# Attention loop of a hybrid decoder layer: TensorE's order fixed to the program's, and each step's first scores written ahead of the transposes of the step behind it

## The chip, the cores and the metric

The kernel runs on one core of one Trainium2 chip. The metric is the device time of one execution in microseconds (us), as the median of several runs. Below, PE is TensorE (PEld its weight loads), DVE is VectorE, ACT is ScalarE, POOL is GpSimd and SP is SyncE.

## What is computed

One layer of a decoder on 1024 tokens of width 1024, in float32: a half-step SwiGLU, then two attentions side by side (MLA and FoX, eight heads each), gated and projected, then a second half-step SwiGLU. The part that the change touches is the attention, swept over blocks of 128 queries:

```python
def one_block(i):
    start = i * Q_BLOCK
    q_blk = lax.dynamic_slice_in_dim(q, start, Q_BLOCK, axis=2)
    logits = jnp.einsum('bhqd,bhkd->bhqk', q_blk, k, preferred_element_type=jnp.float32) * scale
    if log_decay_cum is not None:
        c_q = lax.dynamic_slice_in_dim(log_decay_cum, start, Q_BLOCK, axis=2)
        logits = logits + (c_q[..., :, None] - log_decay_cum[..., None, :])
    logits = jnp.where(k_pos[None, :] <= q_pos[:, None], logits, -jnp.inf)
    probs = jax.nn.softmax(logits, axis=-1)
    return jnp.einsum('bhqk,bhkd->bhqd', probs.astype(v.dtype), v)
...
y_mla = mla_mixer(q_lat, kv_lat, k_rope, ...)
y_fox = fox_mixer(fq, fk, fv, f_logit, ...)
mixed = (jax.nn.sigmoid(g_mla + b_gate[l, 0]) * (y_mla @ w_branch_mla[l])
         + jax.nn.sigmoid(g_fox + b_gate[l, 1]) * (y_fox @ w_branch_fox[l]))
x = x + mixed @ w_o[l]
```

## The kernel before, in words

The layer runs as one program in stages: first SwiGLU, input projection, attention, output projection, second SwiGLU. To keep float32 accuracy with fast matmuls, most operands are split into a high and a low part, and a product is made of two or three matmuls.

**The loop.** `attention` (line 1874) has 64 steps: 2 attentions x 8 heads x 4 groups `g` of two query blocks. A step holds

- the scores of its two query blocks (`scores`, line 2010): matmuls into a tile `pss` (three passes for MLA, two for FoX); DVE adds the causal mask on the diagonal block (line 2025) and takes the maximum (line 2027, `nm`), and ACT makes the exponentials and their sum (line 2030) into a slot of `s_act`. The first block, 2g, is called A below, the second, 2g+1, is called B.
- of the step behind it (`later`, line 2033): `g+1` chunks of transposes of the exponentials (line 2049, PE through an identity into a tile `pspt`, seven or eight matmuls for two chunks). Each chunk is split into high and low by ACT and then DVE (`split_sb`, lines 167 and 170, into `s_v`). Then the product with the values (lines 2059 and 2064, tile `pspv`), which ACT copies out and DVE adds (lines 2066 and 2067, `cmb`), and POOL adds into place. The chunks are called T0 to T3 and the product P.
- 12 matmuls (sometimes 24, in three steps none) of other work with tiles `psgate` and `psg`: the input projection of the two gates and, at the end, the MLA branch's projection. Their operands (`op`, `whi`, `wlo`) are split by ACT and DVE in earlier steps, some from sums that POOL makes.
- now and then a small piece: the forget gates' sums (`chain`), the reciprocal of the sums per pair of heads (`finish_pair`, line 2077), loads of the next head by SP.

**Buffers.** PSUM has two tiles for `pss` (two banks each), a ring of three banks for everything from `psb` (`pspt`, `pspv` and small pieces, in the order in which the program asks for them) and one bank for `psg`. So in a step with four chunks, T0 and T1 take two banks of the ring, T2 takes the bank of the product that just ended, once ACT and DVE have copied it out, and T3 takes T0's bank, once it is split.

**The order of the work.** The program's text gives the order of one step before the change: half of the chunks behind, A, the rest of the chunks, B, gate matmuls and other pieces, P. (With one or two chunks all of them go ahead of A.) But a scheduler sets the order on each engine: it takes what is ready by its own estimate, earlier text first, and so it moves single transposes, scores and gate matmuls past each other. In some other stages the kernel fixes an engine's order to the text's with `in_order` (line 127), which makes each instruction of the named engines follow the one that the text has before it, without a semaphore. The attention loop had no such fix.

Of the kernel before, what the change touches and what calls it, by code (L numbers as in the profile page):

```python
# [10 lines left out]
F32 = mybir.dt.float32  # L11
# [8 lines left out]
P = 128  # L20
T = 1024
NT = T // P
# [5 lines left out]
HEADS = 8  # L28
# [24 lines left out]
class Parts:  # L53
# [5 lines left out]
    def at(self, k, s=slice(None)):  # L59
        return self.tiles[k // self.per][:, k % self.per, s]  # L60
# [5 lines left out]
class Layer:  # L66
# [1807 lines left out]
    def attention(self, gates, more, mix):  # L1874


        nc = self.nc
        vbuf = {}
        pbuf = self.parts("act", 4, 2)
        values = self.slot("act", F16, 4096).rearrange("p (b t c) -> p b t c", b=2, t=NT)  # L1880
        self.pcount = 0
        self.rest = None
        ops = {}
        GR = NT // 2

# [24 lines left out]
        for i in (2, 5, 7, 9):  # L1910
            at(i, lambda: next(chain, None))
        pinned = []
        for k, e in ((k, e) for k in (3, 1, 2, 4) for e in range(2)):
            for f, engine in ((sum_of, None), (high, mybir.EngineType.Activation), (low, mybir.EngineType.DVE)):
                pinned.append((engine, lambda f=f, k=k, e=e: f(k, e)))
        for i in range(2 * HEADS * GR):
            for f in jobs.get(i, ()):
                f()
            k, g = divmod(i, GR)
            a, h = divmod(k, HEADS)  # L1920
            j = h % 2
            if g == 0:
                load(k + 1)
                if j == 0:
                    atp = self.ring.tile([P, T], F32, tag="atp", bufs=2, name="atp")
                    rs = self.sm.tile([P, NT, 2], F32, tag="rsum", bufs=2, name="rsum")
            pr = []
            chunks = late[0] if late is not None else []
            half = len(chunks) // 2 if len(chunks) > 2 else len(chunks)
            for f in chunks[:half]:  # L1930
                f()
            pr.append(self.scores(ops[k], 2 * g, j, rs, pbuf))
            for f in chunks[half:]:
                f()
            pr.append(self.scores(ops[k], 2 * g + 1, j, rs, pbuf))
            if i < 57:
                for engine, f in pinned[2 * i - 2:2 * i] if i else ():
                    last = engine and self.latest(engine)
                    f()
                    if last:  # L1940
                        self.follow(last)
                if i == 11:
                    begin(0)
                if i == 13:
                    sums(0)
                while gates and done < (total - 1) * (i + 1) / 57 + (i > 1):
                    gates.pop(0)()
                    done += 1
                if len(gates) <= 6 and pieces:
                    pieces.pop(0)()  # L1950
                if i == 55:
                    prep()
                if i == 56:
                    sig()
            else:
                for _ in range(2 if i % 2 else 1):
                    if len(mla) > 5:
                        mla.pop(0)()
            if self.rest is not None and (i - 1) % GR == 0:
                scaled = self.rest()  # L1960
                self.rest = None
            if scaled is not None and (i - 3) % GR == 0:
                scaled()
                scaled = None
            if i == 2 * HEADS * GR - 3:
                self.make_sel()
                fox = self.at_slots("v")
                for p in range(2):
                    self.split_at(fox, 1, p)
            if i == 2 * HEADS * GR - 1:  # L1970
                self.split_at(fox, 1, 2)
            if late is not None:
                late[1]()
            late = self.later(a, h, g, j, pr, vbuf[k // 2][:, :, j * P:(j + 1) * P], atp, rs)
# [305 lines left out]
```

## Time and profile before

| | us |
|---|---|
| median of 3 runs (2071.18 to 2074.14) | 2073.53 |
| the profiled execution's own time | 2072.48 |
| its span | 2070.7 |
| PE busy in the span | 2027.4 |
| DVE busy in the span | 1502.1 |
| ACT busy in the span | 1184.6 |
| the attention loop's place in the span | 880 to 1301 |

The profile is that of one execution. Lines such as L2049 are lines of the kernel before; a row names line, engine, operation, what is written and read (`out<-in`, with buffer numbers left out), its shape, how often, and busy us. "idle before" is the engine's idle time ahead of the rows' instructions, and the name behind the arrow is what ended it. Matmuls are pipelined, and their ends in the profile are modelled: the next one starts before the one ahead has ended. The granted clock is the share of full speed that PE was given.

### The profile page before, as it was taken

Reading aid. Unit: us, or ns where it says so; the run is one execution under the profiler, and the core shown is the slowest. Engines: PE = TensorE matmul, PEld = TensorE weight load, DVE = VectorE, ACT = ScalarE, POOL = GpSimd, SP = SyncE. Lnnn points to the kernel's source line nnn. Section 1 sums busy time; section 2 is a strip of 40 time slices with the busy share of each in tenths; the row PEclk is TensorE's granted clock in tenths of the full one; section 3 lists DMA queues with packets and bytes.
Section 4 is the critical chain, followed back from the end, with each engine's and each line's share of the span. In section 5 each row is a group of like instructions: output and inputs, shape, how many; then the busy total and the mean of one; then the engine's idle time right before and its main releaser. Section 6 shows DMA issues by size and latency. Waiting matters only on the chain.

```text
span 2070.7 us, 28667 instructions
## 1 busy us (share of the span) xinstructions
PE 2027.4 (98%) x10187; PEld 1101.0 (53%) x10187; DVE 1502.1 (73%) x2514; ACT 1184.6 (57%) x2005; POOL 691.7 (33%) x748
## 2 busy tenths in 40 slices
PE   8999999999999999999999999999999999999999
PEld 4444444444447555566666666478444444444445
DVE  7866666778877789578888888763765555459876
ACT  6666665545564454467777776422566666555552
POOL 4454544752201212123222321000254555564300
PEclk9999999999999999999999999999999999999999
DMA  8248676575534465654455575541554564355433
GB/s 230 76 143 269 201 250 203 177 270 178 171 110 167 135 195 151 179 137 115 133 140 147 147 211 157 189 147 55 134 144 136 185 181 138 122 197 205 143 111 112
DMA packets 271833, 336.00 MB, mean 162 GB/s; under 512 B 21817, under 2 KB 201897, under 8 KB 271690
## 3 DMA queue, kind: packets, MB, share of 16 engines
q1 hardware_dynamic: 271690, 334.18, 52.8%
q8 instruction: 80, 1.31, 0.3%
q14 instruction: 63, 0.52, 0.1%
HBM read 240.32 MB, written 93.81 MB: 161 GB/s over the span
## 4 chain that ended last, share of the span: by engine, by line
PE 77%; DVE 12%; ACT 5%; issue 3%; DMA 2%; SPq 0%; POOL 0%; ACTq 0%; DVEq 0%; POOLq 0%
PE pst L1104 19%; PE psd L1257 15%; PE psb L1104 11%; PE psg L1104 3%; DVE op L170 2%; PE pss L2023 2%; PE psb L159 2%; PE pspt L2049 2%; PE psb L157 2%; PE psb L158 2%; PE psgate L1104 2%; PE pspv L2059 2%; ACT s_act L2030 1%; PE psin L159 1%; PE psin L157 1%
## 5 line engine op out<-in xcount | busy, mean ns | idle before, releaser
L1104 PEld LDWEIGHTS <-op 128*128 128x128 f16 x3780 | 366.4, 98 | 431.6 <-issue 4.0
L1257 PE MATMUL psd<-op 128*128 128x512 f16 x1680 | 364.3, 379 | 1.2 <-DVE s_wd L209 0.8
L1257 PEld LDWEIGHTS <-op 128*128 128x128 f16 x1680 | 164.3, 98 | 199.8 <-issue 2.6
L170 DVE SCALAR_TENSOR_TENSOR op<-s_u,s_v,op 128x512 f16<-128x512 f32 x170 | 151.4, 900 | 90.1 <-ACT op L167 89.8
L1104 PE MATMUL pst<-s_u,op 128*128 128x512 f16 x720 | 165.2, 379 | 1.3 <-DVE s_act L1152 1.3
L1104 PE MATMUL pst<-s_v,op 128*128 128x512 f16 x720 | 165.2, 379 | 1.3 <-DVE s_u L1152 1.3
L167 ACT ACTIVATE op<-s_u,s_v 128x512 f16<-128x512 f32 x170 | 118.0, 714 | 83.8 <-PE psd L1257 71.6
L170 DVE SCALAR_TENSOR_TENSOR op<-s_act,s_wd,op 128x512 f16<-128x512 f32 x130 | 118.5, 924 | 58.7 <-ACT op L167 58.7
L2030 ACT ACTIVATE s_act<-pss,nm 128x128 f32<-128x128 f32 (+7 forms) x128 | 94.7, 740 | 60.7 <-DVE nm L2027 60.1
L2023 PE MATMUL pss<-s_wd 96*128 96x256 f32 (+5 forms) x480 | 122.8, 372 | 0.5 <-ACT s_act L2030 0.2
L2069 POOL COPY atp<-cmb 64x128 f32<-64x128 f32 x64 | 22.6, 353 | 279.7 <-DVE cmb L2067 275.4
L1073 POOL TENSOR_TENSOR sums<-s_u 128x512 f32<-128x512 f32 x20 | 27.6, 1382 | 252.0 <-PE psa L620 157.1
L2049 PE MATMUL pspt<-ident,s_act 128*128 128x128 f32 x576 | 95.1, 282 | 15.4 <-ACT s_act L2030 10.0
L170 DVE SCALAR_TENSOR_TENSOR s_v<-pspt,s_v 128x512 f16<-128x512 f32 (+1 forms) x160 | 95.4, 629 | 9.4 <-ACT s_v L167 8.6
L2027 DVE TENSOR_REDUCE nm<-pss 128x1 f32<-128x128 f32 (+7 forms) x128 | 95.4, 751 | 2.2
L167 ACT ACTIVATE s_v<-pspt 128x512 f16<-128x512 f32 (+1 forms) x160 | 82.6, 552 | 23.0 <-PE pspt L2049 21.2
L167 ACT ACTIVATE op<-s_wd 128x512 f16<-128x512 f32 x70 | 50.4, 721 | 76.3 <-PE psd L1257 73.1
L167 ACT ACTIVATE op<-s_act,s_wd 128x512 f16<-128x512 f32 x130 | 88.8, 710 | 6.7 <-PE pst L1104 4.1
L2049 PEld LDWEIGHTS pspt<-ident,s_act 128*128 128x128 f32 x576 | 66.2, 142 | 47.1 <-ACT s_act L2030 28.8
L2023 PEld LDWEIGHTS pss<-s_wd 96*128 96x128 f32 (+1 forms) x480 | 78.5, 192 | 8.1 <-ACT s_act L2030 1.8
L1104 PE MATMUL psb<-s_wd,op 128*128 128x512 f16 x360 | 82.6, 379 | 0.0
L1104 PE MATMUL psb<-s_u,op 128*128 128x512 f16 x360 | 82.6, 379 | 0.0
(567 smaller groups left out, 4569.7 us busy)
## 6 DMA issues: line engine op xcount, KB each, us to landing
sumd<-s_u SPq DMA_DIRECT2D x20, 1024.0 KB
s_u<-in_w_in_dram SPq DMA_DIRECT2D x19, 1024.0 KB
s_wd<-in_ffn_w_down_dram SPq DMA_DIRECT2D x32, 512.0 KB
sumd<-s_wd SPq DMA_DIRECT2D x13, 1024.0 KB
s_wd<-fd SPq DMA_DIRECT2D x48, 256.0 KB
s_act<-in_ffn_w_down_dram SPq DMA_DIRECT2D x22, 512.0 KB
s_wd<-sumd SPq DMA_DIRECT2D x14, 768.0 KB
s_u<-sumd SPq DMA_DIRECT2D x14, 768.0 KB
```

The costliest lines, as they stand in the source:

```text
L157: mm(out, lhsT=lh, rhs=rh, start=start, stop=False)
L158: mm(out, lhsT=lh, rhs=rl, start=False, stop=False)
L159: mm(out, lhsT=ll, rhs=rh, start=False, stop=stop)
L167: self.nc.scalar.activation(hi, src, AF.Copy, scale=scale)
L170: self.nc.vector.scalar_tensor_tensor(out=lo, in0=src, scalar=scale, in1=hi, op0=ALU.mult, op1=ALU.subtract)
L1104: mm(out, lhsT=a[:, k, :], rhs=b[:, k, :], start=start and k == 0 and i == 0, stop=k == n - 1 and i == 2, skip_group_check=True,)
L1257: nc.tensor.matmul(o, lhsT=u[:, r], rhs=w, start=start and m == 0, stop=k == CK - 1 and m == 2, skip_group_check=True,)
L2023: mm(ps[:, b:e], lhsT=a[:, q], rhs=bb[:, b:e], start=k == 0, stop=k == len(passes) - 1)
L2027: nc.vector.tensor_reduce(out=nm, in_=ps[:, :n], op=ALU.max, axis=AX.X, negate=True)
L2030: nc.scalar.activation(pn[:, :n], ps[:, :n], AF.Exp, bias=nm, accum_out=rs[:, i, j:j + 1])
L2049: nc.tensor.transpose(pt[:, o:o + P], pr[m][:, kt * P:(kt + 1) * P], self.ident)
L2059: mm(po[:, :256], lhsT=v[:, kt, :], rhs=slab[:, s, c, e * 256:(e + 1) * 256], start=kt == 0 and s == 0, stop=False,)
```

## The change

The whole body of the loop goes under `in_order` for PE. So PE's instructions from the first step's to the last step's stand as in the text; DVE, ACT, POOL and SP are still ordered by the scheduler, which now reckons with this order of PE. And the text is changed in one place: A stands ahead of the first half of the chunks, and B ahead of the rest. (With one or two chunks, all of them stand between A and B.) The rest of the body is only indented. The line numbers behind line 1916 grow by one.

```diff
-        for i in range(2 * HEADS * GR):
-            for f in jobs.get(i, ()):
-                f()
...
+        with self.in_order(mybir.EngineType.PE):
+            for i in range(2 * HEADS * GR):
+                for f in jobs.get(i, ()):
                     f()
...
             pr = []
             chunks = late[0] if late is not None else []
             half = len(chunks) // 2 if len(chunks) > 2 else len(chunks)
-            for f in chunks[:half]:
-                f()
-            pr.append(self.scores(ops[k], 2 * g, j, rs, pbuf))
-            for f in chunks[half:]:
-                f()
-            pr.append(self.scores(ops[k], 2 * g + 1, j, rs, pbuf))
...
+                pr.append(self.scores(ops[k], 2 * g, j, rs, pbuf))
+                for f in chunks[:half]:
+                    f()
+                pr.append(self.scores(ops[k], 2 * g + 1, j, rs, pbuf))
+                for f in chunks[half:]:
+                    f()
```

The first place is on PE, in a step with four chunks in the FoX half, from the end of a product on. Numbers tell the tiles apart: `pss_10579` is A, `pss_10599` is B, and T0 and T1 are `pspt_10565` and `pspt_10572`. Before:

```order
L2064 MATMUL pspv_10535<-s_v_10479,s_act_7781 128x256
L2049 MATMUL pspt_10565<-ident_91,s_act_7780 128x128
L2049 MATMUL pspt_10572<-ident_91,s_act_7780 128x128
L2023 MATMUL pss_10579<-s_wd_10263 128x256
L2023 MATMUL pss_10579<-s_wd_10264 128x256
L1104 LDWEIGHTS op_10458
L1104 MATMUL psgate_10518<-s_u_5345,op_10458 128x512
L1104 LDWEIGHTS op_10458
L1104 MATMUL psgate_10518<-s_u_5346,op_10458 128x512
L1104 LDWEIGHTS op_10458
L1104 MATMUL psgate_10518<-s_u_5345,op_10458 128x512
L2049 MATMUL pspt_10565<-ident_91,s_act_7780 128x128 x3
```

Before, one transpose each of T0 and T1 stood ahead of A, and three gate matmuls between A and the rest of T0. The same place after the change (A is now `pss_10565`, B `pss_10586`, T0 to T3 are `pspt_10572`, `pspt_10579`, `pspt_10593` and `pspt_10600`):

```order
L2065 MATMUL pspv_10535<-s_v_10479,s_act_7781 128x256
L2024 MATMUL pss_10565<-s_wd_10263 128x256
L2024 MATMUL pss_10565<-s_wd_10264 128x256
L2050 MATMUL pspt_10572<-ident_91,s_act_7780 128x128 x4
L2050 MATMUL pspt_10579<-ident_91,s_act_7780 128x128 x4
L2024 MATMUL pss_10586<-s_wd_10263 128x256
L2024 MATMUL pss_10586<-s_wd_10264 128x256
L2050 MATMUL pspt_10593<-ident_91,s_act_7780 128x128 x4
L2050 MATMUL pspt_10600<-ident_91,s_act_7780 128x128 x3
L1104 LDWEIGHTS op_10458
L1104 MATMUL psgate_10518<-s_u_5345,op_10458 128x512
```

Now A, T0, T1, B, T2 and T3 follow each other without anything between them, and all gate matmuls stand behind T3.

The second place is on PE too, in one of the three steps without gate matmuls of their own; the rows start in B (`pss_11016`), and the step's product is `pspv_11025`. Before:

```order
L2023 MATMUL pss_11016<-s_wd_10555 128x512
L2023 MATMUL pss_11016<-s_wd_10556 128x512
L2023 MATMUL pss_11016<-s_wd_10555 128x256
L2023 MATMUL pss_11016<-s_wd_10556 128x256
L1104 LDWEIGHTS op_10907
L1104 MATMUL psgate_11078<-s_u_8215,op_10907 128x512
```

Seven gate matmuls of the next step followed here, and then the product. After the change:

```order
L2024 MATMUL pss_11016<-s_wd_10555 128x512
L2024 MATMUL pss_11016<-s_wd_10556 128x512
L2024 MATMUL pss_11016<-s_wd_10555 128x256
L2024 MATMUL pss_11016<-s_wd_10556 128x256
L2060 LDWEIGHTS s_act_7781
L2060 MATMUL pspv_11025<-s_v_10993,s_act_7781 128x256
```

The product now follows B directly, and the gate matmuls stay in the next step.

The third place is on DVE, around the copy of a product (`cmb`) at the start of a step with four chunks. The rows start with the last split of the step before; `pss_10795` is that step's B, `pss_10868` is A. Before:

```order
L170 SCALAR_TENSOR_TENSOR s_v_10765<-pspt_10789,s_v_10765 128x384
L2025 TENSOR_TENSOR pss_10795<-pss_10795,maskb_5607 128x128
L2027 TENSOR_REDUCE nm_10801<-pss_10795 128x1
L2025 TENSOR_TENSOR pss_10868<-pss_10868,maskb_5607 128x128
L2067 TENSOR_TENSOR cmb_10835<-pspv_10823,cmb_10835 64x512
L2027 TENSOR_REDUCE nm_10872<-pss_10868 128x1
L2084 RECIPROCAL rinv_10933<-rsum_10274 128x8x2
L170 SCALAR_TENSOR_TENSOR op_10816<-sums_10622,ws_97,op_10816 128x512
L170 SCALAR_TENSOR_TENSOR op_10819<-s_act_10462,ws_97,op_10819 128x512
L170 SCALAR_TENSOR_TENSOR s_v_10841<-pspt_10854,s_v_10841 128x512
```

The copy stood ahead of the two gate operands (`op`), and these ahead of T0's split. After the change (`pss_10782` is B of the step before, `pss_10854` is A):

```order
L2028 TENSOR_REDUCE nm_10788<-pss_10782 128x1
L170 SCALAR_TENSOR_TENSOR s_v_10765<-pspt_10798,s_v_10765 128x384
L170 SCALAR_TENSOR_TENSOR op_10816<-sums_10622,ws_97,op_10816 128x512
L170 SCALAR_TENSOR_TENSOR op_10819<-s_act_10462,ws_97,op_10819 128x512
L2085 RECIPROCAL rinv_10933<-rsum_10274 128x8x2
L2026 TENSOR_TENSOR pss_10854<-pss_10854,maskb_5607 128x128
L2068 TENSOR_TENSOR cmb_10835<-pspv_10823,cmb_10835 64x512
L2028 TENSOR_REDUCE nm_10858<-pss_10854 128x1
L170 SCALAR_TENSOR_TENSOR s_v_10841<-pspt_10861,s_v_10841 128x512
```

B's maximum moved ahead of the last split, and the two gate operands moved from behind the copy to ahead of it; T0's split now follows the copy and A's maximum.

More of the change, by code (lines that the diff above doesn't have):

```diff
@@ L1915, in attention @@
                 pinned.append((engine, lambda f=f, k=k, e=e: f(k, e)))
-        for i in range(2 * HEADS * GR):
-            for f in jobs.get(i, ()):
-                f()
[L1919 to L1929, printed above, removed]
-            for f in chunks[:half]:
-                f()
-            pr.append(self.scores(ops[k], 2 * g, j, rs, pbuf))
-            for f in chunks[half:]:
-                f()
-            pr.append(self.scores(ops[k], 2 * g + 1, j, rs, pbuf))
-            if i < 57:
-                for engine, f in pinned[2 * i - 2:2 * i] if i else ():
-                    last = engine and self.latest(engine)
-                    f()
[L1940 to L1974, printed above, removed]
@@ new lines, in attention @@
+        with self.in_order(mybir.EngineType.PE):
+            for i in range(2 * HEADS * GR):
+                for f in jobs.get(i, ()):
+                    f()
+                k, g = divmod(i, GR)
+                a, h = divmod(k, HEADS)
+                j = h % 2
+                if g == 0:
+                    load(k + 1)
+                    if j == 0:
+                        atp = self.ring.tile([P, T], F32, tag="atp", bufs=2, name="atp")
+                        rs = self.sm.tile([P, NT, 2], F32, tag="rsum", bufs=2, name="rsum")
+                pr = []
+                chunks = late[0] if late is not None else []
+                half = len(chunks) // 2 if len(chunks) > 2 else len(chunks)
+                pr.append(self.scores(ops[k], 2 * g, j, rs, pbuf))
[4 more added lines that the diff above has]
+                    f()
+                if i < 57:
+                    for engine, f in pinned[2 * i - 2:2 * i] if i else ():
+                        last = engine and self.latest(engine)
+                        f()
+                        if last:
+                            self.follow(last)
+                    if i == 11:
+                        begin(0)
+                    if i == 13:
+                        sums(0)
+                    while gates and done < (total - 1) * (i + 1) / 57 + (i > 1):
+                        gates.pop(0)()
+                        done += 1
+                    if len(gates) <= 6 and pieces:
+                        pieces.pop(0)()
+                    if i == 55:
+                        prep()
+                    if i == 56:
+                        sig()
+                else:
+                    for _ in range(2 if i % 2 else 1):
+                        if len(mla) > 5:
+                            mla.pop(0)()
+                if self.rest is not None and (i - 1) % GR == 0:
+                    scaled = self.rest()
+                    self.rest = None
+                if scaled is not None and (i - 3) % GR == 0:
+                    scaled()
+                    scaled = None
+                if i == 2 * HEADS * GR - 3:
+                    self.make_sel()
+                    fox = self.at_slots("v")
+                    for p in range(2):
+                        self.split_at(fox, 1, p)
+                if i == 2 * HEADS * GR - 1:
+                    self.split_at(fox, 1, 2)
+                if late is not None:
+                    late[1]()
+                late = self.later(a, h, g, j, pr, vbuf[k // 2][:, :, j * P:(j + 1) * P], atp, rs)
```

## The prediction

> **What bounds the kernel now.** I read the page first, then busy time by window over the attention loop, then TensorE's waits there, then its neighbours' durations, and last the timeline of one step. The page's shares of the span:
>
> ```profile
> PE 2027.4 (98%) x10187; PEld 1101.0 (53%) x10187; DVE 1502.1 (73%) x2514; ACT 1184.6 (57%) x2005; POOL 691.7 (33%) x748
> ```
>
> TensorE (PE) has work almost all the time, so the change can win only what PE waits inside the loop. The loop's first and last scores put it at 880 to 1301 us. The window view for that stretch, with its halves (columns: length, busy us and instructions of PE, PEld, DVE, ACT, POOL, granted clock, DMA share, GB/s):
>
> ```profile
> 880.00:1095.00 215.00, 207.71 (x1260) 140.38 (x1259) 175.27 (x309) 151.95 (x307) 62.05 (x112) 0.99 0.50 132
> 1095.00:1301.00 206.00, 195.25 (x1171) 125.71 (x1169) 171.87 (x296) 144.30 (x290) 51.49 (x106) 0.99 0.59 160
> 880.00:1301.00 421.00, 402.96 (x2428) 266.08 (x2427) 347.14 (x605) 296.25 (x596) 113.54 (x218) 0.99 0.54 146
> ```
>
> PE is idle for 421.00 - 402.96 = 18.0 us. VectorE (DVE) works 347.14 us, 82% of the loop and 83% of its second half, so it is the nearest second bound: even without one PE wait, the loop is not much shorter than DVE's queue plus its latencies. The waits that PE and its weight loader (PEld) show in the loop:
>
> ```profile
> PE pspt L2049 <- ACT s_act L2030: 10.0, 15, 2.0
> PE pspt L2049 <- DVE cmb L2067: 2.8, 4, 1.1
> PE pspt L2049 <- DVE s_v L170: 1.1, 1, 1.1
> PEld pspt L2049 <- ACT s_act L2030: 28.8, 55, 2.2
> PEld pspt L2049 <- DVE cmb L2067: 8.6, 15, 1.3
> PEld pspt L2049 <- DVE s_v L170: 3.0, 8, 0.6
> ```
>
> Nearly every wait stands before a transpose (pspt). Three things end it: the exponentials (ScalarE, s_act), the copy of an older product out of the bank that the transpose needs (cmb), and the split of an older transpose (s_v). PE's rows are too low, because a matmul's modelled end covers the start of a wait: a transpose lasts 282 ns in the group below, but starts 0.11 us behind its neighbour (three in 1142.40 to 1142.73 further down). PEld's rows are too high, because it may idle while PE still works. PE's idle time before transposes (15.4 us, next fence) plus 0.16 us for each of the 55 + 15 + 8 = 78 waits gives 15.4 + 12.5 = 28 us. By PEld's shares, 20 us of that wait for exponentials, 6 for cmb, 2 for s_v.
>
> The durations that the steps below use, from the groups by line within the loop (busy us, mean ns | idle before it and what ended it):
>
> ```profile
> L2049 PE MATMUL pspt<-ident,s_act 128*128 128x128 f32 x576 | 95.1, 282 | 15.4 <-ACT s_act L2030 10.0 <-DVE cmb L2067 2.8 <-DVE s_v L170 1.1
> L170 DVE SCALAR_TENSOR_TENSOR s_v<-pspt,s_v 128x512 f16<-128x512 f32 x96 | 63.0, 682 | 8.0 <-ACT s_v L167 7.4
> L2067 DVE TENSOR_TENSOR cmb<-pspv,cmb 64x512 f32<-64x512 f32 x63 | 43.2, 686 | 17.5 <-ACT cmb L2066 16.5
> L2025 DVE TENSOR_TENSOR pss<-pss,maskb 128x128 f32<-128x128 f32 x128 | 36.2, 290 | 18.3 <-PE pss L2023 17.5 <-ACT s_v L167 0.3
> L170 DVE SCALAR_TENSOR_TENSOR s_v<-pspt,s_v 128x384 f16<-128x384 f32 x64 | 35.1, 548 | 1.5 <-ACT s_v L167 1.2
> L170 DVE SCALAR_TENSOR_TENSOR op<-s_act,ws,op 128x512 f16<-128x512 f32 x25 | 18.5, 755 | 9.8 <-ACT op L167 9.6
> L2027 DVE TENSOR_REDUCE nm<-pss 128x1 f32<-128x128 f32 x16 | 4.6, 286 | 0.3
> L2066 ACT COPY cmb<-pspv 64x512 f32<-64x512 f32 x63 | 36.5, 580 | 16.6 <-PE pspv L2064 15.1 <-POOL s_act L1074 0.2
> ```
>
> **The change, part by part.** It adds and removes no work on PE; it moves it. A and B are a step's first and second scores, T0 to T3 the transposed chunks of the step behind, P the product of the step behind. A step with group g has g chunks behind it, or four when g is 0. Before, one step with four chunks on the timeline of PE (start us, us, what, idle time before it):
>
> ```profile
> 1137.36 0.27 PE L2064 MATMUL pspv<-s_v,s_act 128*128 128x256 f16 x1
> 1137.47 0.38 PE L2049 MATMUL pspt<-ident,s_act 128*128 128x128 f32 x2
> 1137.61 0.48 PE L2023 MATMUL pss<-s_wd 128*128 128x256 f32 x2
> 1139.21 1.58 PE L2049 MATMUL pspt<-ident,s_act 128*128 128x128 f32 x10 [1.12 <-DVE cmb L2067]
> 1140.55 0.49 PE L2023 MATMUL pss<-s_wd 128*128 128x256 f32 x2
> 1140.88 1.69 PE L1104 MATMUL psgate<-s_u,op 128*128 128x512 f16 x7
> 1142.40 0.49 PE L2049 MATMUL pspt<-ident,s_act 128*128 128x128 f32 x3
> 1142.73 1.24 PE L1104 MATMUL psgate<-s_u,op 128*128 128x512 f16 x5
> 1143.81 1.69 PE L2059 MATMUL pspv<-s_v,s_act 128*128 128x256 f16 x14
> 1145.34 0.27 PE L2064 MATMUL pspv<-s_v,s_act 128*128 128x256 f16 x1
> ```
>
> The same step on ACT and DVE (the copy's two halves, and B's exponentials):
>
> ```profile
> 1137.73 0.58 ACT L2066 COPY cmb<-pspv 64x512 f32<-64x512 f32 x1 [0.67 <-PE pspv L2064]
> 1138.33 1.11 ACT L2030 ACTIVATE s_act<-pss,nm 128x1024 f32<-128x1024 f32 x1
> 1138.46 0.69 DVE L2067 TENSOR_TENSOR cmb<-pspv,cmb 64x512 f32<-64x512 f32 x1
> ```
>
> From one product's last matmul to the next product's it takes 1145.34 - 1137.36 = 7.98 us. Starts give the spacing: two narrow scores 0.33 us (1140.55 to 1140.88), a gate matmul 0.217 (seven to 1142.40), a transpose 0.11, a product matmul 0.11 (14 in 1.53).
>
> *Scores ahead of transposes.* The order shows that the scheduler had already put A ahead of all but one transpose of a chunk: of T0 and T1 one each went first, which needs only the first exponentials. Moving those is worth at most 0.11 us each while nothing waits. What is new is that B too passes T1 and T2 in steps of three chunks (seven transposes, 0.77 us), so that B's exponentials are asked for 0.77 us earlier before the next product. Of the 20 us of exponential waits that can take all or nothing; B's maximum and exponentials still queue on a DVE that is 82% busy, so I take a third, -7 us, in the steps of one to three chunks (bounds 0 and -20; those of four come next).
>
> *Gate matmuls no longer fill.* Before, the scheduler put 1 to 12 gate matmuls (0.2 to 2.6 us) between A and the transposes, and between T1 and T3, in many steps of four chunks. Now all stand behind T3, where they cover the product's wait for the splits. I work the quoted step out in the new order, from the product's last matmul: 0.11, A 0.33, so T0 is due at 0.44. It needs the exponentials of the last B, which ended at 1138.33 + 1.11 = 1139.44, 2.08 behind the product; 0.77 earlier is 1.31, with the next DVE or ACT piece perhaps ahead of it. T0 waits 0.87. T0 and T1 take 0.88, B 0.33: T2 is due at 1.31 + 0.88 + 0.33 = 2.52. T2 needs the bank of the product just ended: there are three such banks, and T0 and T1 hold the others. The copy ended at 1138.46 + 0.69 = 1139.15, at 1.79; that is the early end, with no wait. In the new order DVE has two gate operands (0.755 each) queued ahead of that copy, and A's mask as before: 3.3 is the late end, a wait of 0.78. T3 needs T0 split: a split of 0.682 and its ACT half behind T0, or the copy, a maximum (0.286) and the split; I count 0.2 to 0.53 for it. Without waits the step takes 0.11 + 0.33 + 0.88 + 0.33 + T2 0.44 + T3 0.33 + twelve gate matmuls 2.6 + fifteen product matmuls 1.65 = 6.67. With them it takes 6.67 + 0.87 + (0 to 0.78) + (0.2 to 0.53) = 7.7 to 8.85, against 7.98: -0.3 to +0.9. Steps of four chunks that had gate matmuls in these gaps waited less before, and can only lose, up to 1.3. Over 16 such steps: -5 to +18 us. I take +0.45 each, +7 us, near the middle.
>
> *Products without gate matmuls in front.* The pacing leaves three loop steps without gate matmuls. The scheduler had pulled some of the next step's forward there; now P follows its last transposes (or B) directly. The last chunk needs its ACT half and then its DVE half (0.548 or 0.682); with copy, mask or maximum in the queue that is 1 to 2.5 us after the transpose, less B or the product's first matmuls. I take 0.8 us each, +2.5 us (bounds +1 and +5).
>
> *Elsewhere.* Outside the loop the order of PE, ACT, DVE, GpSimd and SyncE is unchanged; inside it, the gate operands keep a step's distance to their matmuls, and the loads of the next head are issued at the same place. Nothing.
>
> Sum: -7 + 7 + 2.5 = +2.5 us. The profiled execution took 2072.48 us (span 2070.7), so 2075 on its scale; it is 1.05 us below the median of the three runs, so **2076 us**. A measurement of this kernel can tell about 0.2%, 4.1 us, from no change.
>
> One rule of the trace has to be priced as well, the clock. Two places with clustered waits, each with the stretch ahead of it:
>
> ```profile
> 920.00:930.00 10.00, 8.01 (x42) 5.62 (x41) 6.81 (x10) 5.05 (x9) 2.27 (x6) 0.88 0.57 148
> 923.50:927.55 4.05, 2.06 (x13) 1.68 (x12) 2.18 (x2) 3.84 (x6) 0.00 (x0) 1.00 0.39 93
> 1208.00:1220.00 12.00, 10.25 (x55) 6.92 (x54) 10.14 (x15) 10.28 (x18) 1.15 (x3) 0.86 0.70 221
> 1137.00:1146.00 9.00, 7.83 (x57) 5.71 (x56) 6.82 (x14) 7.15 (x17) 1.16 (x3) 1.00 0.55 115
> ```
>
> When PE worked 2.06 of 4.05 us, the granted clock then fell (0.88 over 10 us, 0.86 over 12: 1.2 to 1.7 us lost). One wait of 1.1 us, as at 1137 to 1146, left it at 1.00. So waits of about 2 us close together cost 1.7 us more; the waits of T0, T2 and T3 lie within 2.5 us of each other, and reach 2.2 us together only at the late end (0.87 + 0.78 + 0.53). I put nothing in the sum for it. [...]
>
> **Rivals.** *The exponential waits go* (faster). If B's 0.77 us and A's place ahead of every transpose are enough, the 20 us shrink to 4, nothing else is lost in the four-chunk steps, and the gate-less products cost 2: -14 us, 2060. For it: the mean wait, 28.8 / 55 = 0.5 us, is shorter than 0.77. Against it: steps of one and two chunks have nearly the same order as before, and DVE's load is unchanged.
>
> *The bank of the last product* (slower). If the copy regularly ends over 2.5 us after its product (the point from which T2 waits for it whatever the exponentials do), the step that is worked out pays 0.9 and those that had cover up to 1.3; at 1.1 each, 16 x 1.1 = 18, plus 3 for the gate-less products, plus 2 for a fall of the clock, less 5 for exponentials: +18 us, 2091. For it: 8.6 us already wait for cmb on PEld, and the new order puts operand splits ahead of that copy. Against it: DVE idled 17.5 us before its cmb, 16.5 of them for ACT's half, so it is often free by then.
>
> **How the numbers follow.** The forecast, waits moved but hardly fewer, 2067 to 2084: 0.42, of which 0.04 lies over 0.2% faster, 0.30 within, 0.08 slower. The exponential waits go: 0.28, all faster. The bank: 0.30, all slower. So faster 0.32, same 0.30, slower 0.38. The likeliest case's own range is 2067 to 2084; to leave out no more than 2 in 10 the range takes in most of both rivals, 2059 to 2092.
>
> **What would show it.** Right: PE's idle time in the loop again 14 to 24 us, with pspt's wait for s_act down from 10.0 and its waits for cmb and s_v up from 2.8 and 1.1 together to about 8; a pspv wait for s_v that hardly existed. The forecast is wrong if the s_act wait is gone and cmb stays (first rival), or if cmb and s_v grow past 20 us or the clock row shows new falls (second).

## The result, and the profile after

The changed kernel takes 2088.63 us (median of 4 runs, 2086.52 to 2091.04), the kernel before 2073.10 on the same chip (4 runs, 2071.18 to 2074.14). The ratio is 1.0077 (95% interval 1.0065 to 1.0090): slower by 15.5 us, more than the 0.2% that can be told from no change. The range of 2059 to 2092 holds it; the likeliest time, 2076, was 12.6 us too low. The profiled execution took 2089.07 us, its span is 2087.2.

The engines' row on the page:

```profile
PE 2026.5 (97%) x10187; PEld 1105.9 (53%) x10187; DVE 1501.3 (72%) x2514; ACT 1187.9 (57%) x2005; POOL 684.3 (33%) x748
```

The window view of the loop, whose last product now starts at 1317.4 instead of 1301.0 (columns as in the prediction):

```profile
880.00:1316.00 436.00, 401.79 (x2422) 270.57 (x2423) 345.92 (x604) 299.15 (x596) 109.15 (x218) 0.99 0.52 141
```

PE does the same work in 2026.5 instead of 2027.4 us, and the granted clock is 0.99 as before. What grew is PE's idle time in the loop: 436.00 - 401.79 = 34.2 us, against 18.0. The waits of PE and its weight loader in the loop:

```profile
PE pspt L2050 <- ACT s_act L2031: 8.2, 12, 1.5
PE pspt L2050 <- DVE cmb L2068: 7.1, 12, 1.5
PE pspt L2050 <- DVE s_v L170: 4.9, 8, 1.6
PE psg L157 <- DVE s_u L1868: 3.9, 4, 1.2
PE pspv L2060 <- DVE s_v L170: 3.4, 6, 1.1
PE pss L2024 <- DMA s_wd<-mk: 1.9, 1, 1.9
PE pspv L2060 <- DVE cmb L2068: 1.9, 2, 1.0
PE psgate L157 <- ACT z L1770: 1.4, 1, 1.4
...
PEld pspt L2050 <- ACT s_act L2031: 11.7, 13, 1.8
PEld pspt L2050 <- DVE cmb L2068: 11.6, 18, 1.8
PEld pspt L2050 <- DVE s_v L170: 7.9, 15, 1.9
```

The group of the transposes:

```profile
L2050 PE MATMUL pspt<-ident,s_act 128*128 128x128 f32 x576 | 88.0, 279 | 21.5 <-ACT s_act L2031 8.2
```

The exponentials (s_act) hold the transposes 12 times instead of 15, 8.2 us instead of 10.0. The copy of the product (cmb) rose from 2.8 to 7.1, the split (s_v) from 1.1 to 4.9. Four waits are new or nearly so: products (pspv) for splits and copies; gate matmuls for the tile that they write, psg for the reader of the group before and psgate for a tanh (z); and the loop's first scores (pss) for the load of their operands.

Where in the loop? The last matmul of each step's product is a mark that every kernel has, 64 in all, numbered 0 to 63 from here on. Cut at the marks 0, 3, 55 and 63, the loop before gives four stretches in the window view:

```profile
880.00:887.20 7.20, 6.35 (x35) 3.82 (x33) 3.27 (x9) 3.62 (x11) 0.00 (x0) 1.00 1.05 279
887.20:912.49 25.29, 24.44 (x150) 16.40 (x148) 22.99 (x44) 18.06 (x32) 7.50 (x16) 1.00 0.50 126
912.49:1246.36 333.87, 319.93 (x1936) 212.76 (x1934) 274.22 (x476) 241.24 (x490) 95.70 (x176) 0.99 0.56 146
1246.36:1301.03 54.67, 52.27 (x314) 33.12 (x312) 46.65 (x78) 33.33 (x65) 10.35 (x26) 1.00 0.43 133
```

The same four after the change:

```profile
880.00:889.29 9.29, 7.67 (x40) 4.53 (x41) 3.34 (x9) 4.11 (x11) 0.00 (x0) 1.00 1.04 269
889.29:915.86 26.57, 23.91 (x146) 16.16 (x144) 22.94 (x43) 19.15 (x34) 7.15 (x16) 1.00 0.48 117
915.86:1254.47 338.61, 315.65 (x1926) 216.03 (x1924) 273.27 (x475) 242.77 (x489) 90.36 (x176) 0.99 0.53 143
1254.47:1317.38 62.91, 55.94 (x328) 35.09 (x326) 47.15 (x78) 33.23 (x63) 11.64 (x26) 1.00 0.38 117
```

The start is longer by 2.1 + 1.3 = 3.4 us, the 52 middle steps by 4.7, the last eight by 8.2: 16.3 us in the loop. But the marks do not part the same work. The last stretch has 314 matmuls before the change and 328 after it, the middle one 1936 and 1926: the scheduler had drawn 12 gate matmuls (psg) of the last eight steps ahead of mark 55. Counted in the traces, the middle stretch holds 587 gate matmuls before and 576 after, the last one 125 and 137. At 0.217 us each (the spacing in the prediction) the middle steps thus lose about 4.7 + 2.4 = 7.1 us and the last eight about 8.2 - 2.6 = 5.6; these two are estimates. PE's idle time (length less busy) puts the weight in the same places: it grew by 2.6 us at the start, 9.0 in the middle and 4.6 at the end.

So about a third of the loss lies in the last eight steps, an eighth of all. There, four steps (those of marks 56, 58, 60 and 62) have 24 gate matmuls in a row. The middle of one such block on PE's timeline, and below it the one wait inside a block of psgate in the first steps:

```profile
1290.45 0.38 PE L159 MATMUL psg<-s_act,wlo 128*128 128x512 f16 x1
1291.97 0.38 PE L157 MATMUL psg<-s_act,whi 128*128 128x512 f16 x1 [1.13 <-DVE s_u L1868]
...
896.22 0.38 PE L157 MATMUL psgate<-s_u,whi 128*128 128x512 f16 x1 [1.35 <-ACT z L1770]
```

Twelve matmuls make one half of a result in the single psg bank. The next twelve may start only when DVE (or ACT) has read it: from 1290.45 to 1291.97 it takes 1.52 us where neighbours are 0.21 apart. In a fixed order nothing can stand in that gap.

The four-chunk step that the prediction worked out (mark 38 to 39) now reads so on PE:

```profile
1145.84 0.27 PE L2065 MATMUL pspv<-s_v,s_act 128*128 128x256 f16 x1
...
1146.19 1.04 PE L2050 MATMUL pspt<-ident,s_act 128*128 128x128 f32 x8
1146.98 0.49 PE L2024 MATMUL pss<-s_wd 128*128 128x256 f32 x2
1147.68 0.66 PE L2050 MATMUL pspt<-ident,s_act 128*128 128x128 f32 x4 [0.22 <-DVE cmb L2068]
1148.73 0.55 PE L2050 MATMUL pspt<-ident,s_act 128*128 128x128 f32 x3 [0.39 <-DVE s_v L170]
...
1153.23 0.27 PE L2065 MATMUL pspv<-s_v,s_act 128*128 128x256 f16 x1
```

It takes 7.39 us, against 7.98 before and 7.7 to 8.85 foretold. T2 does wait for the copy and T3 for a split, as foretold. But T0 and T1 (the eight at 1146.19) wait for nothing: the exponentials were done before the product.

### The profile page after: what moved, and what is told of

It is laid out like the page before. It is cut to its first block, busy times and chain, and to the rows that moved or that the text cites. A ratio compares the mean times of both kernels' runs of the same rounds, so it can differ in the third digit from the quotient of the medians.

```text
span 2087.2 us, 28636 instructions
## 1 busy us (share of the span) xinstructions
PE 2026.5 (97%) x10187; PEld 1105.9 (53%) x10187; DVE 1501.3 (72%) x2514; ACT 1187.9 (57%) x2005; POOL 684.3 (33%) x748
## 4 chain that ended last, share of the span: by engine, by line
PE 43%; DVE 7%; ACT 2%; issue 2%; POOL 0%; DMA 0%; ACTq 0%; SPq 0%; DVEq 0%
PE pst L1104 9%; PE psd L1257 7%; PE psb L1104 6%; PE psgate L1104 3%; PE psb L157 2%; PE psb L158 2%; PE psb L159 2%; PE pss L2024 1%; PE pspv L2060 1%; DVE op L170 1%; DVE nm L2028 1%; DVE s_v L170 1%; PE pspt L2050 1%; PE psg L1104 1%; PE psg L157 1%
## 5 line engine op out<-in xcount | busy, mean ns | idle before, releaser
L2050 PE MATMUL pspt<-ident,s_act 128*128 128x128 f32 x576 | 88.0, 279 | 21.5 <-ACT s_act L2031 8.2
L2050 PEld LDWEIGHTS pspt<-ident,s_act 128*128 128x128 f32 x576 | 66.3, 141 | 36.9 <-ACT s_act L2031 11.7
```

Of the source, the lines that this page charges most:

```text
L2050: nc.tensor.transpose(pt[:, o:o + P], pr[m][:, kt * P:(kt + 1) * P], self.ident)
```

## The experiments

Times are medians; "before" was timed on the same chip in each group: 2072.54 us for the first four kernels, 2071.93 for the next four, 2071.67 for the last four. Ratios are against it, with their 95% interval. All are compared with the changed kernel's 2088.63. The kernel before differs by up to 1.4 us from group to group (2073.10 to 2071.67), and the intervals of two ratios together leave about 0.2%, some 4 us, open, so a difference between two of these kernels that is smaller than that is not certain.

**The two parts of the change, each alone.** The fixed order with the old text (half of the chunks, A, the rest, B):

```diff
-                pr.append(self.scores(ops[k], 2 * g, j, rs, pbuf))
                 for f in chunks[:half]:
                     f()
-                pr.append(self.scores(ops[k], 2 * g + 1, j, rs, pbuf))
+                pr.append(self.scores(ops[k], 2 * g, j, rs, pbuf))
                 for f in chunks[half:]:
                     f()
+                pr.append(self.scores(ops[k], 2 * g + 1, j, rs, pbuf))
```

> The changed kernel with the old text: half of the chunks, A, the other chunks, B, but PE still fixed to the text. Theory (the fixed order costs, because nothing fills a wait and because groups of gate matmuls in one step follow each other in the single psg bank; the scores' new place helps a little): slower than the changed kernel, 2092 to 2105 us, with PEld's wait of pspt for s_act at 20 us or more. Rival 1 (the scores' new place is what costs, by delaying T2, T3 and the product): back to 2073 to 2080. Rival 2 (only the fixed order matters, the text's order hardly): 2085 to 2091.

It took 2137.62 us (ratio 1.0317, 1.0302 to 1.0332): 65 us slower than before, and slower than every range that was expected. The largest of its waits between the marks 0 and 55 (us in total, times, longest):

```profile
PE pspt L2050 <- ACT s_act L2031: 29.9, 27, 2.6
PE pspt L2050 <- DVE cmb L2068: 16.4, 16, 1.8
```

Its second and third stretch in the window view:

```profile
889.00:919.95 30.95, 26.56 (x147) 17.20 (x145) 22.91 (x43) 19.52 (x34) 6.10 (x16) 0.89 0.43 105
919.95:1300.11 380.16, 329.69 (x1927) 222.10 (x1925) 273.67 (x474) 243.69 (x487) 90.69 (x176) 0.96 0.49 133
```

With the chunks ahead of A, PE stands behind the exponentials for 29.9 us and behind the copy of the product for 16.4 (8.2 and 7.1 in the whole loop of the changed kernel), and its clock falls besides (0.89 and 0.96). So under a fixed order, scores first is worth 2137.62 - 2088.63 = 49 us.

The other part alone, the new text with the order left to the scheduler:

```diff
-        with self.in_order(mybir.EngineType.PE):
-            for i in range(2 * HEADS * GR):
+        for i in range(2 * HEADS * GR):
```

> The kernel before with the new text but without the fixed order: the scheduler still moves PE's instructions. Theory: within 6 us of the kernel before, 2067 to 2079, since the scheduler again fills waits with gate matmuls. Rival 1 (the scores' new place costs by itself): 2083 to 2091.

It took 2062.08 us (2059.97 to 2064.30; ratio 0.9953, 0.9938 to 0.9968): faster than before by 10.5 us, and better than was expected. Its middle stretch:

```profile
915.15:1238.73 323.58, 314.84 (x1936) 215.53 (x1934) 275.56 (x477) 241.81 (x489) 91.37 (x176) 0.99 0.56 150
```

PE's largest wait in the loop, and the largest that is left before transposes:

```profile
PE pspv L2059 <- DVE s_v L170: 2.7, 4, 1.2
...
PE pspt L2049 <- ACT s_act L2030: 1.3, 2, 1.0
```

The change is thus a gain of 10.5 us by its text and a loss of 26.5 by its fixed order (2062.08 to 2088.63). By the stretches, the new text alone is 10.3 us shorter than before in the middle and 0.6 in the last eight steps, but 2.7 longer at the start: from 880 to mark 3 it takes 35.15 us, against 32.49 before and 35.86 after the change. The rest of the experiments ask what the order costs.

**The last eight steps.** The fixed order up to step 55, the last eight steps free:

```diff
+        for part in (range(56), range(56, steps)):
+          with self.in_order(mybir.EngineType.PE) if part[0] == 0 else nullcontext():
+            for i in part:
```

> The changed kernel, but the last eight of the 64 steps are left to the scheduler. Theory (24 gate matmuls in a row in steps 57 to 63 wait for the single psg bank, and the scheduler used to part them): 7 to 9 us less than the changed kernel, 2079 to 2082. Rival (the bank of the last product and T3's split in all 16 four-chunk steps): the two such steps in the last eight are worth 2 us, 2086 to 2088.

2080.78 us (ratio 1.0042, 1.0027 to 1.0057): 7.9 us back, as expected. The waits for psg, copies and exponentials that PE has in the last eight steps of the changed kernel (3.9 + 1.7 + 1.1 = 6.7 us) are gone from its trace. And the fixed order everywhere, with the second group of twelve gate matmuls, in those four steps, moved behind the product:

```diff
-                    for _ in range(2 if i % 2 else 1):
-                        if len(mla) > 5:
-                            mla.pop(0)()
+                    if len(mla) > 5:
+                        mla.pop(0)()
...
                     late[1]()
+                if i >= 57 and i % 2 and len(mla) > 5:
+                    mla.pop(0)()
```

> The changed kernel, but in steps 57, 59 and 61 the second group of 12 gate matmuls stands behind the product instead of directly behind the first group, so that the psg bank has the product's time to be emptied. Theory: PE's wait of psg for s_u falls from 3.9 to below 1 us, and the time by 4 to 7 us, to 2082 to 2085. Rival (the four-chunk steps): no change, 2087 to 2090.

2084.32 us (ratio 1.0062, 1.0045 to 1.0078): 4.3 us back, as expected (from four steps, 63 being the one that the expectation leaves out), and the psg wait fell from 3.9 to 1.5 us. So most of what the last eight steps lose, about 5.6 us, seems to be the wait for the single bank; the 4.3 us are at the edge of what two kernels' times can tell.

**Moving work by hand in the other steps.** Four kernels moved one block to where PE had waited. In steps without gate matmuls (13, 27, 41 and 55 by the mark of their product; there are four, not three), the product behind the next A:

```diff
                 pr.append(self.scores(ops[k], 2 * g, j, rs, pbuf))
+                if pend is not None:
+                    pend()
+                    pend = None
+                had = done
...
+                    if i < 57 and done == had:
+                        pend = late[1]
+                    else:
+                        late[1]()
```

> The changed kernel, but in the four steps without gate matmuls the product stands behind the next step's first scores. In the changed kernel's profile these four products start 4.2 us late in sum. Theory (the fixed order costs where nothing stands between a chunk and its product): the next scores cover 2 to 3 us of it, 2085 to 2087. Rival (the wait moves on to the next transposes): no change, 2088 to 2090.

2095.88 us (2089.75 to 2097.51; ratio 1.0111, 1.0094 to 1.0127): outside both ranges, and slower. In its profiled execution, the fastest of the four, the loop's last mark is at 1318.1, against 1317.4. The place behind mark 40 shows why nothing was won:

```profile
1162.00 1.62 PE L2031 MATMUL pss<-s_wd 128*128 128x512 f32 x4 [1.93 <-ACT s_act L2038]
1163.42 1.50 PE L2067 MATMUL pspv<-s_v,s_act 128*128 128x256 f16 x6
```

The product no longer waits, but A in front of it does, for older exponentials: by the row it is they that still read its pss tile. Why the other three executions were 5.6 to 7.8 us longer than the profiled one is not shown by any trace here.

In steps with four chunks, the block of gate matmuls between B and T2:

```diff
-                for f in chunks[half:]:
+                for f in chunks[half:] if len(chunks) < 4 else ():
                     f()
...
+                for f in chunks[half:] if len(chunks) == 4 else ():
+                    f()
```

> The changed kernel, but in steps with four chunks the gate matmuls stand between B and T2 instead of behind T3. Theory (T2 waits for the bank of the last product and T3 for T0's split, and gate matmuls used to fill that time): PE's waits of pspt for cmb and s_v together fall from 12.0 to below 4 us, and the time by 8 to 12 us, to 2077 to 2081. Rival 1 (the waits only move to the product, which has lost its cover): pspv's wait for s_v rises by as much, 2086 to 2090. Rival 2 (these waits are small next to those of the first steps and the last eight): 2 us, 2086 to 2088.

2095.90 us (ratio 1.0115, 1.0100 to 1.0130): missed, and slower than either theory had it. Two of its waits:

```profile
PE pspv L2062 <- DVE s_v L170: 13.0, 22, 2.1
...
PE pspt L2052 <- DVE s_v L170: 1.6, 1, 1.6
```

The end of the same four-chunk step (mark 38 to 39) on PE's timeline:

```profile
1155.31 0.93 PE L2052 MATMUL pspt<-ident,s_act 128*128 128x128 f32 x7
...
1157.50 0.27 PE L2062 MATMUL pspv<-s_v,s_act 128*128 128x256 f16 x1 [0.39 <-ACT s_v L167]
1158.23 0.73 PE L2062 MATMUL pspv<-s_v,s_act 128*128 128x256 f16 x5 [0.46 <-DVE s_v L170]
```

T2 and T3 now follow each other without a gap, and the split's wait before transposes fell from 4.9 to 1.6 us. The copy's only fell from 7.1 to 6.2, so the two make 7.8 us, where below 4 was expected. And the product stands right behind T3, and its wait for DVE's splits grew from 3.4 to 13.0: the block covers the gap before T2 or the one before P, and not both. Of the 5.0 us by which this loop's last mark lies behind the changed kernel's (1322.41 and 1317.38), 1.7 have passed by mark 0, ahead of the first step that the edit touches.

All three edits together (the second group late, the product later, the block before T2):

> The changed kernel with three edits together: the second group of gate matmuls behind the product in steps 57, 59 and 61, the bare products behind the next first scores, and the gate matmuls ahead of T2 in steps with four chunks. Theory (the fixed order costs nothing by itself, only by what stands uncovered): the gains add up, 2070 to 2075, level with the kernel before. Rival (the waits move on): 2080 or more.

2094.94 us (ratio 1.0114, 1.0092 to 1.0136): the theory missed, the rival's 2080 or more holds. The kernel keeps the psg gain (1.5 us of that wait) and both losses: 11.6 us of products waiting for DVE's splits, 3.2 us of A waiting for exponentials.

A longer chain, in every step: A, the product of the step before the last, the first chunks, B, gate matmuls, the other chunks. The second group of the last eight steps stands behind those, and the small pieces that need a finished pair of heads move a step later with the product (not shown):

```diff
                 pr.append(self.scores(ops[k], 2 * g, j, rs, pbuf))
+                if pend is not None:
+                    pend()
...
-                    late[1]()
+                pend = late[1] if late is not None else None
```

> The fixed order with another text: A, the product of the step before the last, the first chunks, B, the gate matmuls, the other chunks. So every product has its chunks' splits a score behind it, and T1 to T3 stand behind gate matmuls in steps with three and four chunks. Theory: as good as the scheduler's order with scores first, 2060 to 2068. Rival (B's exponentials or DVE's queue set the pace, whatever PE's order): 2075 or more.

2106.08 us (ratio 1.0167, 1.0152 to 1.0182): the theory missed; the rival's 2075 or more holds, but its reason is not shown by this. Products wait 13.8 us for ACT's half of a split and 13.3 us for DVE's: only A stands between the last chunk and its product now, so it is again PE's order that leaves a gap uncovered.

**What the scheduler does that the text does not.** In the free order, gate matmuls stand two here, four there, in several gaps of a step. Four kernels were to tell what in that matters. First, the fixed order with the fill spread by hand: in steps with four chunks three gate matmuls between B and T2, two or three between T2 and T3, the rest behind T3; with three chunks four or six between T1 and T2. (`cut` is called after every matmul, or every three, of a gate product, and issues a chunk when `laid` has reached its number.)

```diff
+                if not spread:
+                    for f in chunks[half:]:
+                        f()
+                elif len(chunks) == 3:
+                    chunks[1]()
+                    self.cuts = [(4, chunks[2])]
+                else:
+                    self.cuts = [(3, chunks[2]), (5, chunks[3])]
...
+    def cut(self, n=1):
+        self.laid += n
+        while self.cuts and self.laid >= self.cuts[0][0]:
+            self.cuts.pop(0)[1]()
```

> The new text, TensorE's order fixed over the whole loop, but the 12 gate matmuls of a step are spread by hand: in steps with four chunks, three gate matmuls stand between B and T2, two or three between T2 and T3, the rest behind T3; in steps with three chunks four (or six) stand between T1 and T2. The last eight steps are as in the changed kernel. Theory (the fixed order costs because one block of gate matmuls covers one gap only, where the scheduler shares it out between two or three gaps of the same step): about 10 of the 20 us of waits before transposes go and the product's waits hardly grow, 2070 to 2079 us. Rival (what is lost is moving work across the border between steps): the waits only move again, 2084 to 2094.

2081.23 us (2080.92 to 2082.20; ratio 1.0047, 1.0032 to 1.0062): 7.4 us back, 2 us short of what was expected. Its middle stretch:

```profile
917.69:1246.63 328.94, 311.55 (x1927) 215.63 (x1924) 272.62 (x475) 241.65 (x489) 90.66 (x176) 0.99 0.56 149
```

Its waits before products and transposes, the largest (for exponentials, 7.6 us) left out:

```profile
PE pspv L2078 <- DVE s_v L171: 4.1, 8, 1.1
...
PE pspt L2068 <- DVE cmb L2086: 3.0, 3, 1.5
PE pspt L2068 <- DVE s_v L171: 2.7, 2, 2.4
```

The middle stretch is 9.7 us shorter than the changed kernel's 338.61, with the same 576 gate matmuls in it. It is 4.9 shorter than that of before, or 2.5 when the 11 gate matmuls that it holds fewer are reckoned in; the last eight steps, which this edit leaves alone, keep their loss (62.85 against 62.91). The waits for cmb and s_v before transposes fell from 12.0 to 5.7, and the products' wait for DVE's split rose by only 0.7.

Second, the order fixed within each step but not from one step to the next:

```diff
-        with self.in_order(mybir.EngineType.PE):
-            for i in range(2 * HEADS * GR):
+        for i in range(2 * HEADS * GR):
+            with self.in_order(mybir.EngineType.PE):
```

> The new text, with TensorE's order fixed within each step but not from one step to the next: scores and transposes of the next step may pass the product of this one, and the gate matmuls stay in one block inside their step. Theory of shared-out fill: the cost stays for the most part, 2076 to 2087 us. Rival (moving across the border between steps is what matters): nearly as fast as the free order, 2062 to 2070.

2092.66 us (ratio 1.0100, 1.0085 to 1.0115): outside both ranges, 4 us slower than the whole loop in one chain. The rival, that work must cross the border between steps, gets no support: in some twenty steps scores did cross it here (a transpose in only one), and nothing was won; the next kernel settles it. Why this one is slower still was not followed up. Its granted clock over the marks 0 to 3 was 0.94, the changed kernel's 1.00, but the next kernel has 0.94 there too and is fast.

Third, the counterpart: scores, transposes and products fixed over the whole loop, gate matmuls left out of the chain (`freed` notes the instructions that a gate group issues):

```diff
-            if e not in engines:
+            if e not in engines or i.name in free:
...
-                        gates.pop(0)()
+                        self.freed(gates.pop(0), free)
...
-                            mla.pop(0)()
+                            self.freed(mla.pop(0), free)
```

> The new text, with the order of the scores, transposes and products on TensorE fixed over the whole loop, but the gate matmuls (those of psgate and, in the last eight steps, of psg) left to the scheduler. Theory of shared-out fill: nearly the free order's time, 2061 to 2068 us, since the fixed attention matmuls cost nothing by themselves. Rival (attention matmuls must cross the border between steps): 2078 to 2088.

2065.66 us (2063.27 to 2067.21; ratio 0.9967, 0.9953 to 0.9981): as the theory of shared-out fill had it. Its middle and last stretch:

```profile
915.22:1240.56 325.34, 315.36 (x1935) 217.11 (x1933) 274.51 (x475) 241.00 (x489) 91.48 (x176) 0.99 0.56 148
1240.56:1295.45 54.89, 53.35 (x319) 34.37 (x317) 46.75 (x78) 32.88 (x63) 10.79 (x26) 1.00 0.45 136
```

The same four-chunk step (mark 38 to 39) on PE's timeline:

```profile
1134.32 0.27 PE L2071 MATMUL pspv<-s_v,s_act 128*128 128x256 f16 x1
...
1136.23 0.39 PE L1109 MATMUL psgate<-s_u,op 128*128 128x512 f16 x1
1136.49 0.66 PE L2056 MATMUL pspt<-ident,s_act 128*128 128x128 f32 x4
1136.98 0.59 PE L1109 MATMUL psgate<-s_u,op 128*128 128x512 f16 x2
1137.54 0.55 PE L2056 MATMUL pspt<-ident,s_act 128*128 128x128 f32 x3
1137.93 1.89 PE L1109 MATMUL psgate<-s_u,op 128*128 128x512 f16 x8
...
1141.18 0.27 PE L2071 MATMUL pspv<-s_v,s_act 128*128 128x256 f16 x1
```

One gate matmul stands before T2, two between T2 and T3, eight before P (the twelfth, among T0 and T1, is in the part left out), and no row shows a wait: 6.86 us, against 7.39. Of the fixed order's 26.5 us, 2088.63 - 2065.66 = 23.0 are thus the fixed place of the gate matmuls. The other 3.6 are left for the attention's own matmuls, and these are not clear of the noise: the ratios' intervals, 0.9938 to 0.9968 and 0.9953 to 0.9981, overlap. The two traces point the same way, though: PE's waits before products, for both halves of the split, are 6.0 + 2.3 = 8.3 us here and 2.7 + 2.4 = 5.1 in the free order. By the stretches, the gate matmuls' part is 338.61 - 325.34 = 13.3 us in the middle, 8.0 in the last eight steps and 0.6 at the start (21.9 in the loop); 9 gate matmuls, some 2 us, stand ahead of mark 55 here and behind it in the changed kernel, so nearer 15 and 6.

Last, the new text in the free order, with the second group of gate matmuls of the last eight steps behind the product:

> The new text without the fixed order, and in the last eight steps the second group of 12 gate matmuls is written behind the product. With the free order the wait for the single psg bank was 0.3 us in all, so the theory expects the time of the free order unchanged, 2060 to 2064 us. If the group still costs something there (steps 57, 59 and 61), up to 4 us less, 2057 to 2060.

2062.36 us (2061.71 to 2063.49; ratio 0.9956, 0.9941 to 0.9971): the same as the new text alone, as expected. What helped in the fixed order is worth nothing where the scheduler may part the two groups itself. The new text in the free order remains the best version, faster than both kernels.

## Why the prediction was partly right and partly wrong

The time lies in the range, near its upper end, but not by the mechanism of the forecast: the range is so wide because it takes in most of a rival whose cause did not come. Two terms of the sum failed, the -7 us for the scores and the nothing for all else: the middle steps lost about 7.1 us where the sum has 2.5, and the first and last steps about 9 more.

- **The bound.** Right: the change moved no work, and the whole difference is PE's idle time in the loop, 18.0 to 34.2 us. The expected 14 to 24 was too little.
- **Scores ahead of transposes, -7.** Not borne out in the steps where it was to be won. By the prediction's own way of counting, the 46 waits before transposes make 21.5 + 46 x 0.16 = 28.9 us, and by PEld's shares (11.7, 11.6 and 7.9 of 31.2) 10.8 of that are for exponentials, 9 less than 20. But PE's own row fell only from 10.0 to 8.2, and in the 39 middle steps of one to three chunks PE's idle time rose from 9.1 to 15.2 us; 2.6 of that stands before the bare products of marks 13 and 41. Wrong also in what it is worth by itself: the text alone gave -10.5 in the free order, and 49 us separate the two texts in the fixed one. The prediction weighed A's move against the scheduler's order, in which A was first already, and did not ask what a fixed order would do with the old text.
- **Gate matmuls no longer fill, +7.** Right in the mechanism, wrong in the place. The waits for cmb and s_v rose from 8 to 18 us by the same counting, +10 (from 3.9 to 12.0 in PE's rows). But the four-chunk steps, for which +0.45 each was worked out, lost little. The sum of the times between marks over the 13 such steps in the middle stretch (the step that ends at mark 7, and every fourth from there) is 93.4 us after the change, 96.5 before; they hold 132 gate matmuls instead of 155, and 23 x 0.217 = 5.0 us of work thus stand elsewhere. So they lost about 1.9 us, 0.15 each, and PE's idle time in them rose from 4.8 to 7.8 us. The working had the copy right (it ended at 1.79 behind the product, and in the trace after at 1.78), and was wrong on the exponentials, which it moved by 0.77 us and which were done before the product. The steps with three chunks paid most: 109.8 us against 102.6 over their 13, with 10 gate matmuls more, so a loss of about 5.0. The prediction counted them among the gains, though they too had gate matmuls between their transposes.
- **Products without gate matmuls, +2.5.** Right. There are four such steps instead of three, and of the 3.4 + 1.9 = 5.3 us that PE waits before products (0.5 in the trace of before), 2.9 stand in them.
- **Elsewhere, nothing.** This failed. The first steps are 3.4 us longer, and the last eight lost about 5.6; the prediction looked at neither. In the last eight, 24 gate matmuls came to stand in a row, with one bank for both halves. That the free order had parted such groups was in the order of instructions before; the wait for psg was 0.8 us there, and 3.9 after. The runs show it twice: 4.3 us came back when the second group was moved, 7.9 when the last eight steps were left free. In the first steps a row of 24 waits 1.4 us too, and the first scores wait 1.9 us for their load. Before, gate matmuls stood ahead of them until 880.55; in the fixed order the last one ahead of them starts at 878.29. But this is not the whole of it: with the gate matmuls left free, the loop still takes 35.22 us to mark 3, and 35.15 in the free order with the new text, against 32.49 before. So most of the 3.4 us comes with the text, and why was not traced.
- **The clock.** Nothing in the sum, and nothing came: 0.99 in the loop before and after.
- **The rivals.** The time is nearest to that of the bank of the last product (2091), but that is not what happened. Its own sign was more than 20 us of waits for cmb and s_v, or new falls of the clock; the waits on PE are 12.0 (18 by the prediction's counting), the clock is 0.99, and the four-chunk steps did not pay the 1.1 us each on which it rested. The exponential waits did not go under the fixed order; they did in the free order (1.3 us), where that rival's 2060 is close to the measured 2062.

What stays open: what the new text costs in the first steps, where the up to 3.6 us of the attention matmuls' own fixed order are lost, beyond the longer waits before products, and the extra loss when each step is its own chain.

## What to carry to other kernels

A change that fixes an engine's order and rewrites the text has two effects; cost each alone, since here they were -10.5 and +26.5 us. Filler work that depends on nothing near by was worth most here in small pieces in several gaps (7.4 us back when it was spread by hand, 23.0 when it was left free): a fixed block covered one gap and moved the wait to the next (ahead of T2, it brought the products' wait for DVE's splits from 3.4 to 13.0 us). So fix the order of the chain that matters, if any, and leave the filler out of it. Where a scheduler may carry work from one step to the next, count the work in each stretch, or compare idle time, before saying which steps lost. Before saying that nothing happens elsewhere, look in the order for places where two groups with a single buffer now stand next to each other, above all in the first and last steps, where the pattern of the work differs.

## What the hardware showed that was not expected

The granted clock cost much in one of these loops without one long wait. With the fixed order and the old text it was 0.89 over 30.95 us and 0.96 over 380.16, which is 0.11 x 30.95 + 0.04 x 380.16 = 19 us of lost full-speed time at most; in that loop PE's longest wait was 2.6 us, the waits are only close together. One of the falls in that trace, with the 3.41 us ahead of it (columns as before):

```profile
1194.34:1197.75 3.41, 0.94 (x5) 0.72 (x6) 1.55 (x2) 1.95 (x5) 1.57 (x4) 1.00 0.86 204
1197.75:1201.16 3.41, 3.41 (x13) 3.02 (x12) 2.66 (x5) 1.80 (x4) 3.25 (x3) 0.50 0.02 5
```

PE worked only 0.94 of 3.41 us, around two waits of 1.64 and 1.43, and for the next 3.41 us it was granted half the clock. The loops of the kernel before and of the changed one have two falls each, of 3.41 us at 0.50. In the 3.41 us ahead of them PE worked 1.81 and 1.66 us in the trace of before, 1.43 and 1.88 in the trace after. In these five places PE had thus worked for a quarter to a little over half of the 3.41 us ahead of the fall. Which length or spacing of waits brings a fall is not shown by this.
